# A delta rule kernel: the 4x4 diagonal blocks of a triangular inverse by shuffles and elementwise products in place of 32x32 matmuls

## The chip, the cores and the metric

One core of one Trainium2 chip runs the whole program. The metric is the time of one execution on the device in microseconds. The instructions of an engine run in the order in which they stand; the engines wait for each other by semaphores.

## The reference

The reference is one inference step of a trunk of two layers over 640 tokens (512 latent, 128 prompt). Each layer makes one projection whose columns feed three token mixers (a gated delta rule in both directions, an HGRN2 in both directions, windowed attention), merges the three, and ends in a gated MLP with a convolution. The change touches the delta rule, 4 heads of 128, by chunks of 64 tokens:

```python
decay = _masked_exp(incl, gc[..., :, None] - gc[..., None, :])
kb = k * beta[..., None]
m = jnp.where(strict, jnp.einsum('nbhid,nbhjd->nbhij', kb, k) * decay, 0.0)
t_inv = lax.linalg.triangular_solve(eye + m, jnp.broadcast_to(eye, m.shape),
                                    left_side=True, lower=True, unit_diagonal=True)
u = t_inv @ (v * beta[..., None])
w = t_inv @ (kb * jnp.exp(gc)[..., None])
...
v_new = u_n - jnp.einsum('bhck,bhkv->bhcv', w_n, s)
o = jnp.einsum('bhck,bhkv->bhcv', qg_n, s) + jnp.einsum('bhcs,bhsv->bhcv', qk_n, v_new)
s = s * jnp.exp(gl_n)[..., None, None] + jnp.einsum('bhck,bhcv->bhkv', kd_n, v_new)
```

## The kernel before

The main stream is the projection. It computes 128 columns for all 640 tokens at a time (a tile), from eight steps over the 1024 inputs (`k_steps`, L969; `mtile`, L976); each step is three pairs of fp32r matmuls of 256 and 384 columns, `mm<-hh,whi`, `mm<-hl,whi` and `mm<-hh,wlo`, since activations and weights are each split into a high and a low part. ScalarE (ACT) makes the high part of a weight tile, VectorE (DVE) the low part `wlo`, while the tile before is used. The side streams are generators that run beside it: two delta streams (`delta`, L1281; stream w = 0 takes batches 0, 2, 4, stream w = 1 batches 1 and 3; a batch below 4 is one head of the latent tokens, batch 4 all heads of the prompt), the HGRN streams, attention, and more. Their PSUM tiles are named `sd`, their SBUF slots `ex` and `sl`, their small tiles `sc_...`; `Cv`, `V`, `S` belong to the convolution that follows the projection of a delta head.

No scheduler of a compiler orders this. The planner (`drive`, L512; `step`, L500) keeps its own estimate of when each engine comes free (`_go`, L286, with a cost for each kind of instruction) and places a side stream's next piece, up to its `yield`, when its inputs are estimated to be there; else it places the next step of the main stream. Pieces of the convolutions wait in `aux` and are placed by `pump`. So the order in which every engine works is fixed when the program is built, and depends on the estimated costs. A stream can wait for an event or for free slots (`wait`, `room`); while the main stream waits, only side streams are placed. It waits at three kinds of places; the one after the last tiles of the mixer's projection is

```python
yield from c_tiles()
yield self.wait(("D", l, 0), ("D", l, 1))
```

(L2088 and L2089): both delta streams must have ended before it computes the gates.

In `delta` the inverse of each chunk's triangle, forward and backward at once, is built by doubling blocks, in 32x32 blocks that sit on the diagonal of 128 partitions (L1364 to L1399). `ath` holds the masked products of k with k and the decay, `XC` and `XTC` the inverse so far and its transpose. Blocks of two are made on DVE by a masked product with `bs` (beta of the token and its neighbour). Then four steps make blocks of 4, 8, 16 and 32; each is sixteen 32x32 matmuls, a masked product on DVE (L1388), sixteen more, a transpose and two subtractions on DVE:

```python
for i in range(1, 5):
    ...
    self.mul(phc..., pp..., bc(self.C(C_CP, 2)[:, 32 * i + 32:32 * i + 64], 1, 4))
    ...
    self.vtr(small, px)
    self.sub(yt, yt, blocks(px, m))
    self.sub(e, e, blocks(small, m))
```

Blocks of 64 follow with ACT copies between PE groups (L1401 to L1440). Then, in a batch below 4, a scan over four chunks goes from PE to DVE (`stt`, L371), to PE, to ACT, to PE, to DVE; batch 4 has no scan. `finish_tokens` (L1530) ends a batch: four squares on ACT, a reciprocal root of 4 elements a partition in eleven DVE instructions, a product over 512 columns, and four transposes on PE that need it.

Of the kernel before, what the change touches and what calls it, by code (L numbers as in the profile page):

```python
# [12 lines left out]
ALU = mybir.AluOpType  # L13
# [39 lines left out]
C_I, C_ONE, C_MISC, C_UI, C_LI, C_LS, C_US, C_CP, C_COS = 0, 1, 2, 3, 4, 5, 6, 7, 9  # L53
# [8 lines left out]
def shape_constants():  # L62
    c = np.zeros((128, N_CST), np.float32)
    p = np.arange(128)
    s, t = p[:, None], p[None, :]

    def put(i, a):
        c[:, i * 128:i * 128 + a.shape[1]] = a

    put(C_I, s == t)  # L70
    put(C_ONE, np.ones((128, 128)))
    put(C_UI, s <= t)
    put(C_LI, s >= t)
    put(C_US, s < t)
    put(C_LS, s > t)
    t32 = np.arange(32)[None, :]
    put(C_CP, np.concatenate([s % 32 == t32] + [(s % 32 // (2 << i) == t32 // (2 << i)) & (s % 32 >> i != t32 >> i)
                                                for i in range(5)], 1))
    misc = np.zeros((128, 128), np.float32)
    misc[:64, 2] = 1.0  # L80
    misc[64:, 3] = 1.0
    misc[:, 40] = p % 2 == 0
    misc[:, 41] = p % 2 == 1
    for g in range(4):
        for j in range(16):
            misc[32 * g + j, 8 + j] = 1.0
    for j in range(4):
        for e in range(2):
            misc[32 * j + e, 24 + 2 * j + e] = 1.0
    put(C_MISC, misc)  # L90
    nf = 16
    inv = (np.float32(10000.0) ** (-np.arange(nf, dtype=np.float32) / np.float32(nf))).astype(np.float32)
    pos = np.arange(TS)
    row, col = (pos // 64).astype(np.float32), (pos % 64).astype(np.float32)
    ang = np.where((p % 64 < 32)[:, None], row[None, :], col[None, :]).astype(np.float32) * inv[p % 16][:, None]
    put(C_COS, np.cos(ang.astype(np.float32)))
    put(C_SIN, np.sin(ang.astype(np.float32)) * np.where(p % 32 < 16, -1.0, 1.0).astype(np.float32)[:, None])
    return c
# [120 lines left out]
def bc(ap, axis, n):  # L219

    d = [list(x) for x in ap.ap]
    d.insert(axis, [0, n])
    return bass.AP(ap.tensor, ap.offset, d)
# [13 lines left out]
class Trunk:  # L237
# [325 lines left out]
    def setup(self):  # L563
# [13 lines left out]
        self.c_us, self.c_ls = C(C_US), C(C_LS)  # L577
        self.c_blk, self.c_pick = C(C_MISC)[:, 2:34], C(C_MISC)[:, 24:32]
        self.c_sum = C(C_MISC)[:, 8:24]
        self.c_par = C(C_MISC)[:, 40:42]  # L580
        self.hh = self.hp.tile([128, KD, T], F32R, name="hh")
        self.hl = self.hp.tile([128, KD, T], F32R, name="hl")
        self.S = [self.const.tile([128, 648], F32, name=f"S{j}") for j in range(2)]
# [696 lines left out]

    def delta(self, l, w, batches):  # L1281
        sc, nc = dict(self.sc), self.nc
        for name in ("ssk", "nk", "rk", "b0", "bs", "cq", "ss"):
            sc[name] = self.sc[name][:, w]
        sl = (self.extra, self.slots)
        P, X, XT, kd = (self.pair(*sl) for _ in range(4))
# [1 line left out]
        ath, ph = View(P, 0), View(P, 1)  # L1288
# [3 lines left out]
        for b in batches:  # L1292
# [27 lines left out]
            self.rsqrt(rk, ssk, nk)  # L1320
            self.mul(nk, ssk, rk)
            self.mul(ssk, rk, rk)
            b0 = sc["b0"]
            self.mul(b0, beta, bc(ssk, 1, 2))

            bs = sc["bs"]
# [41 lines left out]
            self.zero(x64)  # L1368
            XC, XTC = (xs.ap[:, o:o + 256].rearrange("p (d n) -> p d n", d=2) for o in (0, 256))
            c32, t32 = (a.rearrange("p d (c x) -> p d c x", c=4) for a in (XC, XTC))  # L1370
            self.mul(t32, bc(bc(self.C(C_CP)[:, 0:32], 1, 4), 1, 2), bc(b0, 3, 32))
            for g in range(4):
                r = slice(32 * g, 32 * g + 32)
                self.mul(phc[r].rearrange("p (c x) -> p c x", c=4), ath.c4[r, :, r], bc(self.C(C_CP)[r, 32:64], 1, 4))
            self.mul(c32, bc(phc.rearrange("p (c x) -> p c x", c=4), 1, 2), bc(bs, 3, 32))
            self.sub(XTC, XTC, XC)
            self.vtr(xs.ap[:, 0:256], xs.ap[:, 256:512])
            yield None
            for i in range(1, 5):
                m = 1 << i  # L1380
                pp = self.psd()[:, 0:128]
                e = mix(XC, m, 0)
                yt = mix(XTC, m, 1)
                for c in range(4):
                    for g in range(4):
                        r = slice(32 * g, 32 * g + 32)
                        self.mm(pp[r, c * 32:(c + 1) * 32], ath.c4[r, c, r], mix_chunk(e, c, m)[r])
                self.mul(phc.rearrange("p (c x) -> p c x", c=4), pp.rearrange("p (c x) -> p c x", c=4),  # L1388
                         bc(self.C(C_CP, 2)[:, 32 * i + 32:32 * i + 64], 1, 4))
                yield None  # L1390
                px = self.psd()[:, 0:128]
                for c in range(4):
                    for g in range(4):
                        r = slice(32 * g, 32 * g + 32)
                        self.mm(px[r, c * 32:(c + 1) * 32], phc[r, c * 32:(c + 1) * 32], mix_chunk(yt, c, m)[r])
# [3 lines that stand above are left out]
                yield None  # L1399
# [507 lines left out]
    def mixer(self, l, x):  # L1907
# [12 lines left out]
        sc = self.sc = {}  # L1920
        for name, shape in (("ab", [2, 2, 5, 4]), ("beta", [2, 5, 4]), ("g", [2, 5, 4]), ("gl", [2, 5, 4]), ("t0", [2, 5, 4]), ("t1", [2, 5, 4]),
                            ("t2", [2, 5, 4]), ("ex", [3, 2, 5, 4]), ("neg", [2, 5, 4]), ("ssk", [2, 4]), ("nk", [2, 4]), ("rk", [2, 4]),
                            ("b0", [2, 2, 4]), ("bs", [2, 2, 4]), ("cq", [2, 4]), ("ss", [2, 3, 4]), ("ssb", [3, 4]), ("ck", [3, 10]),
                            ("s8", [3, 5, 8]),
                            ("mx", [4]), ("ng", [4]), ("es", [4]), ("sm", [4])):
            sc[name] = mp.tile([128] + shape, F32, name="sc_" + name)
# [401 lines left out]
```

## Time and profile before

| what | us |
|---|---|
| median of three runs | 2674.06 |
| lowest and highest | 2673.45, 2674.49 |
| the profiled execution's own time | 2671.22 |
| its span, first to last instruction | 2669.4 |
| PE busy | 2634.9 |
| DVE busy | 1843.0 |
| ACT busy | 1130.8 |
| POOL busy | 114.4 |

The granted clock of TensorE was 1.000 over the whole span. The profile has a page with the busy time of each engine, the chain of work that ended last and the costliest groups; beside it, views of the trace answer for one stretch, one line or one group. In the rows, `x` gives how many records stand in one row; a 32x32 or 128x128 matmul of fp32 has two records, so a group of sixteen stands as x32. What stands in square brackets at a row's end is how long the engine was idle before it, and for whom it waited.

### The profile page before, as it was taken

What the parts mean: (1) busy time and instruction counts of PE and PEld (TensorE: products, weight loads), DVE (VectorE), ACT (ScalarE), POOL (GpSimd) and SP (SyncE); (2) the same over time, 40 slices, a digit from 0 to 9 for tenths busy, and PEclk for the clock granted to TensorE, in tenths of its full rate; (3) what the DMA queues carried; (4) which work ended last, traced back from release to release, by engine and by line L of the source; (5) the groups of instructions that cost most, each with busy time, mean ns of one, the idle gap of its engine ahead of it and who ended that gap; (6) DMA issues with size and microseconds to landing.
All of it is one profiled execution on the core that took longest, in us unless ns stands there. A gap on an engine that the chain in (4) does not pass through costs nothing.

```text
span 2669.4 us, 58665 instructions
## 1 busy us (share of the span) xinstructions
PE 2634.9 (99%) x23938; PEld 2534.1 (95%) x23938; DVE 1843.0 (69%) x4250; ACT 1130.8 (42%) x2577; POOL 114.4 (4%) x208
## 2 busy tenths in 40 slices
PE   8999999999999999999999999999999999999999
PEld 5999999999999999999999998999999999999999
DVE  6788865656765897988667888666564457546454
ACT  5555455544424432323345554645443334323232
POOL 1100110100000000000001001000000000000000
PEclk9999999999999999999999999999999999999999
DMA  8212222312444344444322112222222232222222
GB/s 270 73 40 58 65 75 80 112 53 60 134 132 131 100 141 154 151 149 148 108 77 75 44 49 63 65 71 66 56 64 68 76 115 68 77 74 69 83 74 81
DMA packets 365245, 243.49 MB, mean 91 GB/s; under 512 B 18069, under 2 KB 339137, under 8 KB 364848
## 3 DMA queue, kind: packets, MB, share of 16 engines
q1 hardware_dynamic: 355632, 213.70, 27.7%
q0 software_dynamic: 8912, 25.53, 2.9%
q8 instruction: 188, 3.08, 0.5%
q14 instruction: 81, 0.66, 0.1%
q10 hardware_dynamic: 432, 0.52, 0.1%
HBM read 225.79 MB, written 13.89 MB: 90 GB/s over the span
## 4 chain that ended last, share of the span: by engine, by line
PE 88%; DVE 7%; ACT 2%; issue 2%; DMA 1%; SPq 0%; ACTq 0%; DVEq 0%
PE mm L323 73%; PE sd L323 12%; PE sd L328 2%; DVE sl L358 1%; DVE ex L358 1%; DVE Cv L371 1%; ACT sl L348 1%; DMA ar<-in_ada_w_dram 1%; DVE acc L371 1%; DVE wlo L358 1%; DMA wraw<-in_w_up_dram 0%; DVE N L371 0%; SPq L433 0%; ACT ex L348 0%; DVE x L371 0%
## 5 line engine op out<-in xcount | busy, mean ns | idle before, releaser
L323 PE MATMUL mm<-hh,whi 128*128 128x256 f32 (+2 forms) x3696 | 868.7, 319 | 1.4 <-issue 0.7
L323 PE MATMUL mm<-hl,whi 128*128 128x256 f32 (+2 forms) x3696 | 840.4, 311 | 1.2 <-DVE hl L371 1.2
L323 PE MATMUL mm<-hh,wlo 128*128 128x256 f32 (+1 forms) x3632 | 834.8, 309 | 0.0
L323 PEld LDWEIGHTS mm<-hh,whi 128*128 128x128 f32 (+1 forms) x3696 | 646.1, 187 | 23.8 <-issue 15.4
L323 PEld LDWEIGHTS mm<-hl,whi 128*128 128x128 f32 (+1 forms) x3696 | 663.7, 187 | 4.0 <-DVE hl L371 1.8
L323 PEld LDWEIGHTS mm<-hh,wlo 128*128 128x128 f32 x3632 | 661.7, 188 | 0.0
L358 DVE TENSOR_TENSOR wlo<-wraw,whi 128x512 fp32r<-128x512 f32 x598 | 401.8, 681 | 302.6 <-ACT whi L348 301.8
L348 ACT ACTIVATE whi<-wraw 128x512 fp32r<-128x512 f32 x602 | 366.8, 618 | 306.7 <-PE mm L323 245.6
L371 DVE SCALAR_TENSOR_TENSOR Cv<-S,V,Cv 128x642 f32<-128x642 f32 x240 | 210.9, 886 | 2.3
L371 DVE SCALAR_TENSOR_TENSOR acc<-ar,cT,acc 128x512 f32<-128x512 f32 x252 | 176.8, 749 | 4.2 <-DMA ar<-in_ada_w_dram 4.0
L348 ACT ACTIVATE sl<-sl 128x512 f32<-128x512 f32 (+5 forms) x220 | 117.6, 545 | 143.5 <-DVE sl L358 103.3
L323 PE MATMUL mm<-fh,whi 128*128 128x256 f32 (+1 forms) x704 | 166.0, 311 | 1.8 <-DVE x L371 1.0
L323 PE MATMUL mm<-fl,whi 128*128 128x256 f32 (+1 forms) x704 | 165.0, 309 | 0.2
L323 PE MATMUL mm<-fh,wlo 128*128 128x256 f32 (+1 forms) x704 | 165.1, 309 | 0.0
L348 ACT ACTIVATE sl<-sd 128x512 f32<-128x512 f32 (+5 forms) x216 | 94.4, 451 | 161.7 <-PE sd L323 79.6
L323 PE MATMUL sd<-sl,sl 128*32 128x32 f32 (+4 forms) x3392 | 151.2, 228 | 6.3 <-DVE sl L358 5.1
L323 PEld LDWEIGHTS sd<-sl,sl 128*32 128x32 f32 (+3 forms) x3392 | 126.1, 129 | 26.8 <-issue 13.9
L358 DVE TENSOR_TENSOR sl<-sl,sl 128x512 f32<-128x512 f32 (+2 forms) x212 | 149.0, 741 | 3.3 <-ACT sl L348 2.0
L348 ACT ACTIVATE S<-mm 128x512 f32<-128x512 f32 x204 | 77.8, 434 | 155.0 <-PE mm L323 154.8
L371 DVE SCALAR_TENSOR_TENSOR x<-mm,mod,x 128x256 f32<-128x256 f32 (+1 forms) x192 | 74.6, 434 | 88.2 <-PE mm L323 83.8
L323 PEld LDWEIGHTS mm<-fh,whi 128*128 128x128 f32 x704 | 128.0, 189 | 4.2 <-issue 2.9
L323 PEld LDWEIGHTS mm<-fl,whi 128*128 128x128 f32 x704 | 128.1, 188 | 0.7 <-DVE fl L358 0.7
(280 smaller groups left out, 3121.6 us busy)
## 6 DMA issues: line engine op xcount, KB each, us to landing
wraw<-in_w_in_dram SPq DMA_DIRECT2D x264, 256.0 KB, 3.0
ar<-in_ada_w_dram SPq DMA_DIRECT2D x176, 256.0 KB, 3.5
wraw<-in_w_up_dram SPq DMA_DIRECT2D x176, 256.0 KB, 3.0
wraw<-in_w_down_dram SPq DMA_DIRECT2D x64, 256.0 KB, 3.0
wraw<-in_w_branch_dram SPq DMA_DIRECT2D x48, 256.0 KB, 3.0
wraw<-in_w_out_dram SPq DMA_DIRECT2D x32, 256.0 KB, 3.6
wraw<-in_w_down_dram SPq DMA_DIRECT2D x32, 192.0 KB, 2.6
x<-xspill POOLq DMA_DIRECT2D x16, 320.0 KB, 7.0
```

Source lines behind the costliest of these rows:

```text
L323: self.nc.tensor.matmul(out, lhsT, rhs, start=start, stop=stop)
L328: self.nc.tensor.transpose(out, in_, self.c_i[:k, :k])
L348: self.nc.scalar.activation(out=out, in_=in_, func=func, scale=scale, bias=bias, **kw)
L358: self.nc.vector.tensor_tensor(out, a, b, op=op)
L371: self.nc.vector.scalar_tensor_tensor(out=out, in0=a, scalar=s, in1=b, op0=op0, op1=op1)
```

## The change

The first of the four doubling steps, from blocks of two to blocks of four, is done on DVE without a matmul. The masks of the first two levels are applied in one product (`two`) to a copy of the diagonal blocks, one reduction sums it to 16 numbers a partition (`r4`), and shuffles between lanes, masks by a lane's parity in pairs (`c_pair`) and products of 4 or 8 elements (`q4`, `l4`, `z4`) make the block's four corner numbers (`zt`), which two products spread over 32 columns. The loop of matmuls begins with blocks of eight. Two masks and two constant columns are added, in tiles that the program loads already.

```diff
@@ shape_constants
-    put(C_CP, np.concatenate([s % 32 == t32] + [(s % 32 // (2 << i) == t32 // (2 << i)) & (s % 32 >> i != t32 >> i)
-                                                for i in range(5)], 1))
+    facing = [(s % 32 // (2 << i) == t32 // (2 << i)) & (s % 32 >> i != t32 >> i) for i in range(5)]
+    put(C_CP, np.concatenate([s % 32 == t32] + facing + [facing[1] & (s // 2 % 2 == d) for d in range(2)], 1))
...
+    misc[:, 42] = p // 2 % 2 == 0
+    misc[:, 43] = p // 2 % 2 == 1
@@ delta
-        for name in ("ssk", "nk", "rk", "b0", "bs", "cq", "ss"):
+        for name in ("ssk", "nk", "rk", "bo", "bs", "r4", "q4", "l4", "z4", "cq", "ss"):
             sc[name] = self.sc[name][:, w]
...
-            b0 = sc["b0"]
+            b0, off = sc["bo"][:, 0], sc["bo"][:, 1]
             self.mul(b0, beta, bc(ssk, 1, 2))
...
-            self.mul(t32, bc(bc(self.C(C_CP)[:, 0:32], 1, 4), 1, 2), bc(b0, 3, 32))
+
+            one = ph.ap[:, 256:384].rearrange("p (c x) -> p c x", c=4)
+            two = ph.ap[:, 0:256].rearrange("p (c i x) -> p c i x", c=4, i=2)
             for g in range(4):
                 r = slice(32 * g, 32 * g + 32)
-                self.mul(phc[r].rearrange("p (c x) -> p c x", c=4), ath.c4[r, :, r], bc(self.C(C_CP)[r, 32:64], 1, 4))
-            self.mul(c32, bc(phc.rearrange("p (c x) -> p c x", c=4), 1, 2), bc(bs, 3, 32))
+                self.vcopy(one[r], ath.c4[r, :, r])
+            self.mul(two, bc(one, 2, 2), bc(self.C(C_CP)[:, 32:96].rearrange("p (i x) -> p i x", i=2), 1, 4))
+            self.mul(t32, bc(bc(self.C(C_CP)[:, 0:32], 1, 4), 1, 2), bc(b0, 3, 32))
+            r4, (own, far), l4, z4 = sc["r4"], (sc["q4"][:, i] for i in range(2)), sc["l4"], sc["z4"]
+            self.rsum(r4.rearrange("p c i j -> p (c i) j"), ph.ap[:, 0:256].rearrange("p (a n j) -> p a j n", a=8, j=2))
+            self.mul(c32, bc(two[:, :, 0], 1, 2), bc(bs, 3, 32))
+            self.add(z4[:, 0, :, 0], r4[:, :, 0, 0], r4[:, :, 0, 1])
+            self.sub(XTC, XTC, XC)
+            self.stt(off, bc(z4[:, 0, :, 0], 1, 2), -1.0, bs, ALU.mult, ALU.mult)
+
+            a4, o4, u4 = r4[:, :, 1], z4[:, 1], z4[:, 2:4]
+            self.shuffle(o4, a4, [i ^ 1 for i in range(32)])
+            for t, m in ((far, 1), (own, 0)):
+                self.ts(t, sc["bo"][:, :, 0], self.c_pair[:, m:m + 1], ALU.mult)
+            for t, m in ((far, 0), (own, 1)):
+                self.stt(t, sc["bo"][:, :, 1], self.c_pair[:, m:m + 1], t, ALU.mult, ALU.add)
+            for j in range(2):
+                self.shuffle(l4[:, j], far, [i & 28 | (i & 2 ^ 2) + j for i in range(32)])
+            zz, zt = z4[:, 0], z4[:, 4]
+            self.mul(zz, a4, bc(own[:, 0], 2, 2))
+            self.mul(o4, o4, bc(own[:, 1], 2, 2))
+            self.add(zz, zz, o4)
+            for kind in range(2):
+                self.mul(u4[:, kind], zz, l4[:, :, kind].rearrange("p j c -> p c j"))
+            (ps_, pn_), (s1, _), (s2, _), (s0, _) = u4.ap
+            self.add(zt, u4[:, 0], bass.AP(u4.tensor, u4.offset + s1 + s0, [[ps_, pn_], [s2, 4], [-s0, 2]]))
+            for d in range(2):
+                self.mul(c32[:, d].rearrange("p c (n j) -> p c n j", j=2), bc(zt, 2, 16),
+                         bc(self.C(C_CP, 2)[:, 192 + 32 * d:224 + 32 * d].rearrange("p (n j) -> p n j", j=2), 1, 4))
             self.sub(XTC, XTC, XC)
             self.vtr(xs.ap[:, 0:256], xs.ap[:, 256:512])
             yield None
-            for i in range(1, 5):
+            for i in range(2, 5):
...
```

The planner counts the new instructions, so it sets another order in both layers, though none of its rules is edited. Three places follow, each as the order of the program lists it: line, operation, output and inputs, shape, and how many follow each other. First DVE, layer 0, first batch, the head of the inverse (`ex_684` before and `ex_688` after hold `XC` and `XTC`). Before:

```order
L358 TENSOR_TENSOR ex_684<-cst,sc_b_667 128x256
L358 TENSOR_TENSOR ex_692<-ex_692,cst 32x128 x4
L358 TENSOR_TENSOR ex_684<-ex_692,sc_bs 128x256
L358 TENSOR_TENSOR ex_684<-ex_684 128x256
L387 STREAM_TRANSPOSE ex_684<-ex_684 128x256
```

After, from the same place, the first twelve rows:

```order
L384 COPY ex_696<-ex_696 32x128 x4
L360 TENSOR_TENSOR ex_696<-ex_696,cst 128x256
L360 TENSOR_TENSOR ex_688<-cst,sc_bo 128x256
L410 TENSOR_REDUCE sc_r_668<-ex_696 128x16
L360 TENSOR_TENSOR ex_688<-ex_696,sc_bs 128x256
L360 TENSOR_TENSOR sc_z_671<-sc_r_668 128x4
L360 TENSOR_TENSOR ex_688<-ex_688 128x256
L373 SCALAR_TENSOR_TENSOR sc_bo<-sc_z_671,sc_bs 128x8
L394 STREAM_SHUFFLE sc_z_671<-sc_r_668 128x8
L378 TENSOR_SCALAR sc_q_669<-sc_bo,cst 128x8 x2
L373 SCALAR_TENSOR_TENSOR sc_q_669<-sc_bo,cst,sc_q_669 128x8 x2
L394 STREAM_SHUFFLE sc_l_670<-sc_q_669 128x8 x2
```

All of the new piece stands in one run on DVE, with no instruction of another stream in it.

Second PE, layer 1, the end of the delta streams (`sl_...` and `ex_...` are their slots, `cst` the unit matrix of a transpose). Before, the last row of a delta stream is a transpose of `finish_tokens` among main matmuls, 246 main matmuls ahead of the wait at L2089:

```order
L323 MATMUL mm<-hh,wlo 128x256
L323 MATMUL mm<-hh,wlo 128x384
L328 MATMUL sd_73<-cst,ex_15685 128x128 x4
L323 MATMUL mm<-hh,whi 128x256
L323 MATMUL mm<-hh,whi 128x384
```

After, the last twelve rows of a run of 44 rows (186 matmuls) that stands at that wait, and the main matmul behind it:

```order
L325 MATMUL sd_75<-sl_15559,ex_19517 128x128 x2
L325 MATMUL sd_72<-ex_19516,sl_15576 128x128 x2
L325 MATMUL sd_73<-ex_15617,sl_15568 128x128 x2
L325 MATMUL sd_74<-sl_15559,ex_19517 128x128 x2
L325 MATMUL sd_74<-st_15578,sl_15565 128x128
L325 MATMUL sd_74<-ex_15617,sl_15565 128x128 x3
L325 MATMUL sd_75<-ex_15617,sl_15565 128x128 x3
L325 MATMUL sd_75<-st_15578,sl_15565 128x128
L325 MATMUL sd_72<-ex_19516,sl_15576 128x128 x8
L330 MATMUL sd_73<-cst,sl_15569 128x128 x4
L330 MATMUL sd_74<-cst,sl_15559 128x128 x4
L325 MATMUL mm<-hh,whi 128x256
```

The end of batch 3's scan, its outputs and its transposes moved from among the main matmuls to behind the last of them.

Third PE, layer 0, where the main stream waits for slots. Before, the end of a run of 24 rows (66 matmuls) without a main matmul, and what follows:

```order
L323 MATMUL sd_75<-st_654,sl_648 128x128
L323 MATMUL sd_72<-ex_4080,ex_689 128x128 x4
L323 MATMUL sd_73<-ex_4080,ex_689 128x128 x4
L323 MATMUL sd_74<-sl_634,ex_3836 128x128 x2
L323 MATMUL mm<-hh,whi 128x256
```

After, the end of the like run, of 30 rows (94 matmuls):

```order
L325 MATMUL sd_75<-st_654,sl_648 128x128
L325 MATMUL sd_72<-ex_4102,ex_693 128x128 x8
L325 MATMUL sd_73<-sl_634,ex_3818 128x128 x2
L325 MATMUL sd_74<-ex_3817,sl_651 128x128 x2
L330 MATMUL sd_75<-cst,sl_635 128x128 x4
L330 MATMUL sd_72<-cst,sl_644 128x128 x4
L325 MATMUL mm<-hh,whi 128x256
```

The transposes of an HGRN batch's `finish_tokens` (`sl_635`), which stood after further main matmuls, now stand ahead of them, twelve 128x128 matmuls behind the batch's last product.

## Rows read from the trace of the kernel before

**Rows 1.** The page: busy time by engine, and the chain that ended last.
```profile
PE 2634.9 (99%) x23938; PEld 2534.1 (95%) x23938; DVE 1843.0 (69%) x4250; ACT 1130.8 (42%) x2577; POOL 114.4 (4%) x208
...
PE 88%; DVE 7%; ACT 2%; issue 2%; DMA 1%; SPq 0%; ACTq 0%; DVEq 0%
```

**Rows 2.** Stretches of layer 1's mixer: stretch, its length, busy us (instructions) by engine.
```profile
1540.00:1600.00 60.00, 58.18 (x954) 53.80 (x954) 54.86 (x146) 32.82 (x82) 4.43 (x7) 1.00 0.18 47
1600.00:1660.00 60.00, 57.19 (x748) 53.94 (x750) 51.08 (x144) 28.12 (x68) 9.31 (x17) 1.00 0.24 65
1720.00:1780.00 60.00, 60.00 (x685) 57.65 (x685) 38.58 (x101) 28.40 (x70) 5.31 (x10) 1.00 0.31 85
```

**Rows 3.** Waits of PE from 1480 to 1830 us: total us, times, longest.
```profile
PE sd L323 <- DVE sl L358: 5.0, 3, 1.8
```

**Rows 4.** Timeline: start us, length us, engine, line, operation, tiles, shape, count.
```profile
113.32 0.46 PE L323 MATMUL mm<-hh,wlo 128*128 128x256 f32 x2
...
113.71 0.45 PE L323 MATMUL sd<-ex,ex 32*32 32x32 f32 x32
...
114.09 0.56 PE L323 MATMUL mm<-hh,whi 128*128 128x256 f32 x2
114.24 0.29 DVE L358 TENSOR_TENSOR ex<-sd,cst 128x128 f32<-128x128 f32 x1
...
114.49 0.46 PE L323 MATMUL mm<-hl,whi 128*128 128x256 f32 x2
...
114.79 0.46 PE L323 MATMUL mm<-hh,wlo 128*128 128x256 f32 x2
...
115.70 0.32 DVE L387 STREAM_TRANSPOSE ex<-sd 128x128 f32<-128x128 f32 x1 [0.37 <-PE sd L323]
...
115.94 0.25 DVE L358 TENSOR_TENSOR ex<-ex,sd 128x128 f32<-128x128 f32 x1
...
116.12 0.28 DVE L358 TENSOR_TENSOR ex<-ex,ex 128x128 f32<-128x128 f32 x1
```

**Rows 5.** Groups of DVE by shape: count, busy us, mean ns, idle before.
```profile
L358 DVE TENSOR_TENSOR ex<-ex,cst 32x128 f32<-32x128 f32 x40 | 11.2, 281 | 0.4
...
L358 DVE TENSOR_TENSOR sl<-sl 128x256 f32<-128x256 f32 x14 | 5.9, 422 | 0.1
...
L382 DVE COPY ex<-ex 32x128 f32<-32x128 f32 x24 | 5.2, 218 | 0.3
...
L404 DVE TENSOR_REDUCE sc_mx<-sd 128x1 f32<-128x128 f32 x16 | 3.5, 283 | 0.6 <-PE sd L323 0.6
...
L392 DVE STREAM_SHUFFLE sc_bs<-sc_b 128x8 f32<-128x8 f32 x10 | 1.6, 160 | 0.0
```

**Rows 6.** Timeline of DVE, the reciprocal root of layer 0's first batch.
```profile
94.59 0.16 DVE L376 TENSOR_SCALAR sc_ssk<-sc_ssk 128x4 f32<-128x4 f32 x1
...
97.36 0.17 DVE L358 TENSOR_TENSOR sc_b<-sc_beta,sc_ssk 128x8 f32<-128x8 f32 x1
```

**Rows 7.** Timeline: a scan step and the end of a batch in layer 1.
```profile
1700.03 0.60 ACT L348 ACTIVATE ex<-sd 128x512 f32<-128x512 f32 x1 [2.06 <-PE sd L323]
...
1700.88 0.75 PE L323 MATMUL sd<-sl,ex 128*128 128x128 f32 x4 [0.45 <-DVE sl L371]
...
1701.16 0.32 ACT L348 ACTIVATE ex<-ex 128x128 f32<-128x128 f32 x1
...
1704.85 0.69 DVE L358 TENSOR_TENSOR ex<-ex,sc_ss 128x512 f32<-128x512 f32 x1
```

**Rows 8.** Timeline of PE in layer 0, the stretch without main matmuls.
```profile
353.16 1.04 PE L328 MATMUL sd<-cst,sl 128*128 128x128 f32 x8
...
360.60 2.17 PE L323 MATMUL sd<-sl,sl 128*128 128x128 f32 x18
362.61 0.39 PE L323 MATMUL sd<-st,sl 128*128 128x128 f32 x2
...
364.99 0.54 PE L323 MATMUL mm<-hh,whi 128*128 128x256 f32 x2
```

More of the change, by code (lines that the diff above doesn't have):

```diff
@@ L579, in setup @@
         self.c_sum = C(C_MISC)[:, 8:24]
-        self.c_par = C(C_MISC)[:, 40:42]
+        self.c_par, self.c_pair = C(C_MISC)[:, 40:42], C(C_MISC)[:, 42:44]
         self.hh = self.hp.tile([128, KD, T], F32R, name="hh")
@@ L1922, in mixer @@
                             ("t2", [2, 5, 4]), ("ex", [3, 2, 5, 4]), ("neg", [2, 5, 4]), ("ssk", [2, 4]), ("nk", [2, 4]), ("rk", [2, 4]),
-                            ("b0", [2, 2, 4]), ("bs", [2, 2, 4]), ("cq", [2, 4]), ("ss", [2, 3, 4]), ("ssb", [3, 4]), ("ck", [3, 10]),
+                            ("bo", [2, 2, 2, 4]), ("r4", [2, 4, 2, 2]), ("q4", [2, 2, 2, 4]), ("l4", [2, 2, 2, 4]), ("z4", [2, 5, 4, 2]), ("bs", [2, 2, 4]), ("cq", [2, 4]), ("ss", [2, 3, 4]), ("ssb", [3, 4]), ("ck", [3, 10]),
                             ("s8", [3, 5, 8]),
```

## The prediction

> **What bounds the kernel now.** I read the page's busy shares and its chain first [rows 1]. TensorE (PE) is busy 2634.9 of 2669.4 us, about 34 us are idle, and PE makes 88% of the chain that ended last, DVE 7%. So a PE instruction taken away counts at nearly its whole length, and DVE time counts only where it makes PE wait. Next I read the engines by stretch, in layer 1's mixer, where the delta streams, the HGRN streams and the conv taps all want DVE [rows 2]: PE is busy 58.18 and 57.19 of 60 us there, DVE 54.86 and 51.08 (91% and 85%); DVE is the second bound there, with only 5 to 9 us free in 60. By 1720 to 1780 us PE is full (60.00) and DVE down to 38.58: there the delta streams are done and the projection runs alone. In 1480 to 1830 us PE waits three times for one DVE line's products, 5.0 us in all, 1.8 the longest [rows 3]. That is the price of DVE being late today.
>
> **Removed from PE.** One step of the inverse has two groups of sixteen 32x32 matmuls, over 10 batches (two layers of five): 20 groups. A group that stands alone between main matmuls [rows 4]: the pair before it starts at 113.32, the group at 113.71, the next pair at 114.09 and the one after at 114.49, so 1.17 us for two pair distances, where an undisturbed pair follows the next at 0.30 (114.49 to 114.79). It costs 1.17 - 0.60 = 0.57 us. A group with another small group on both sides gives back only its own 0.38 from start to start (113.71 to 114.09). Twenty of them are 7.6 to 11.4 us; most stand alone among main matmuls, so I take **-10.5 us**.
>
> **Added to and removed from DVE.** Removed per batch: the masked product, the transpose and the two subtractions of that step, 0.29 + 0.32 + 0.25 + 0.28 = 1.13 us [rows 4], and four masked products of 32x128 that become four copies: 281 to 218 ns each, 0.25 us in all [rows 5]. Added: two more 128x256 element operations (the masked doubles, the second subtraction) at 0.42 each, two 128x128 ones at 0.28, the reduction, and fifteen operations on 4 or 8 elements a partition. The reduction of 256 elements has no row: one of 128 elements takes 283 ns [rows 5], twice that is 0.57, and I take 0.42, since a 128x256 operation of the other kind takes that. The fifteen have their neighbours in the reciprocal root of the same batch: 14 operations start between 94.59 and 97.36, 0.198 us each [rows 6], though each lasts only 0.16 to 0.17; the shuffle among them lasts 160 ns [rows 5]. So 0.84 + 0.56 + 0.42 + 15 x 0.2 = 4.8 us are added, 1.4 removed: **+3.4 us of DVE a batch, 34 us in all**, which is not time of the kernel as long as PE has other rows ahead.
>
> An operation on 8 elements a partition takes 160 ns and one on 256 takes 422 [rows 5]: 32 times the elements for 2.6 times the time, so nearly all of a small one is fixed cost. [...]
>
> **What moves.** The delta chain of one batch gets longer: the old step took 113.71 to 116.40, 2.7 us with its waits [rows 4], the new piece 4.8 - 0.25 = 4.6 us of DVE back to back, so at least 2 us a batch. The planner answers with another order, and the order is where the money is.
> Layer 1: before, the last PE row of a delta stream stands 246 main matmuls (some 37 us at 0.30 a pair) ahead of the point where the main stream waits for both delta streams (L2089). After, both streams' last batches (batch 4 in w = 0, batch 3 in w = 1) are still going there: 44 PE rows, 186 matmuls, stand with not one main matmul between them. PE works in order and the whole projection is queued behind these rows, so each dependence in this block is idle time. I walked it by rows. Its PE work is some 20 us (90 of the matmuls are 128x128; nine fp32 ones, two records each, take 2.01 us from 360.60 to 362.61 [rows 8], 0.22 apiece, and transposes less). The waits:
> (a) two transposes at the end of a batch wait for `finish_tokens`: the squares start on ACT at 1701.16, the normed product is done at 1704.85 + 0.69, so 4.4 us, and the copy or add before it is another 0.6 to 0.7, 5.05 us from the last product to the transpose [rows 7]. Batch 4's has 0.95 us of other PE rows in between, idle 4.0; batch 3's has 0.4 (the last rows before the projection goes on), idle 4.7.
> (b) batch 3's scan, three and a half steps of matmul, DVE or ACT, matmul: the trace shows 0.45 us of PE idle for one such wait, though other work stood between [rows 7]; eight of them are 3.6.
> (c) the tail of the inverse, ACT copies between 32x32 and 64x64 groups: 0.65 + 1.25 + 0.6, about 2.5.
> Together 14.8; with 12 if the streams overlap better than I walked them and 18 if DVE is also behind on arrival, **+15 us**.
> Layer 0: the main stream is blocked for slots near main matmul 1376 in a block of 94 matmuls; before, a like block of 66 ran from 353.16 to 364.99 with no idle in it [rows 8]. In the new block the HGRN transpose at its end has 2.8 us of PE work (twelve 128x128 matmuls) between it and the last product it depends on, and needs the same 5.05: **+2.3 us** (1 to 4).
> Elsewhere DVE is late a little more often, or, with the deltas moved, the three waits of layer 1 [rows 3] go: -3 to +6, I take 0.
> Everything after main matmul 9440 (attention, merge, FFN) has the same order; nothing there. The wider constant masks and the new small tiles add no instruction of weight: the constants come in the one load that is there.
>
> **The sum**: -10.5 + 15 + 2.3 = +6.8 us against the profiled run's own 2671.22 us. The profiled run lies 2.8 us under the median of the runs; so the sum added to the median gives **2680.9 us**.
>
> **Rivals.** *Same time*: the block's idle is only 10 to 11 and layer 0's one, since in the block both streams' rows alternate better than in my walk (ACT and DVE run ahead, main work no longer competes for them). Then -10.5 + 11 + 1 = +1.5, 2675.6. For it: during the block DVE has no weights to split, so its queue is short. Against: (a) alone is 8.7 and is a chain of 4 squares on ACT and 13 DVE instructions, which no free engine shortens.
> *Faster*, one mechanism: the three DVE waits in layer 1 [rows 3] go with the shifted streams and the block is covered. Its place is the wait at L2089: if the rows of batch 4 and 3 reach PE with their operands ready (the chains having run ahead on DVE and ACT while main matmuls still filled PE, so that only PE work is left), the block costs its PE work alone, which was to be done anyhow. Then -10.5 + 2 for what is left of the waits and -2 for layer 1's three, or 2663.6. The deciding point is whether batch 3's scan starts before the block; in the order its first scan row stands in the block, hence the low chance.
> *Clearly slower*: DVE saturates. In layer 1's mixer 5 delta batches bring 17 us of DVE to stretches that have 5 to 9 free in 60 [rows 2]; if the order leaves them in about 100 us, 3 to 6 us more of PE waits come, and the block starts with DVE behind, 18: -8 + 18 + 4 + 4 = +18, 2692. [...]
> *The change does not do what it says*: PE's count of 32x32 groups would stay; the order shows 20 groups fewer, so this is out.
>
> **How the numbers follow.** Forecast (2678 to 2686): 0.45. Same: 0.28. Clearly slower (2686 to 2694): 0.15. Faster: 0.12. The measurement tells about 0.2% (5.3 us) from no change, so under 2668.7 is faster and above 2679.4 slower. The forecast's lower edge falls under that line; with it slower is 0.58, same 0.30, faster 0.12. The range leaves out the faster rival and the far end of the slower one: 2668.5 to 2690.
>
> **What would show it.** In the profile after: 320 fewer 32x32 matmuls, which are 640 records, ten reductions of 128x256, some +34 us of DVE busy; a stretch of about 35 us late in layer 1's mixer with no `mm` record and PE busy about 20 of it, two idle pieces of 4 to 5 us in it ending on a transpose that waited for DVE; PE busy in total about 10 us less. Wrong would be: the stretch there with under 8 us idle (then the same or faster rival), or PE waits spread over the whole mixer (then DVE is the bound).

## The result, and the profile after

The changed kernel takes 2703.64 us (median; 2702.01 to 2706.21) where the kernel before takes 2674.27 in the same comparison: a ratio of 1.0113, interval 1.0099 to 1.0128, so about 30 us slower. Its profiled execution has a span of 2700.8 us, 31.4 more than before, at a mean granted clock of 0.994 (1.000 before).

The page of the changed kernel, its busy times by engine and the chain that ended last, answers [rows 1]:

```profile
PE 2640.6 (98%) x23298; PEld 2539.8 (94%) x23298; DVE 1867.5 (69%) x4440; ACT 1131.5 (42%) x2579; POOL 114.7 (4%) x208
...
PE 79%; DVE 10%; ACT 3%; issue 2%; DMA 0%; DVEq 0%; ACTq 0%; SPq 0%
```

PE's idle time, span less busy, went from 34.5 to 60.2 us: +25.7. And PE's busy time did not fall with the 640 records that went; it rose by 5.7. Both have to be explained. Windows of the changed kernel (stretch, its length, busy us and instructions by engine; the third number from the right is the granted clock) answer [rows 2]: the place in layer 0 where the main stream is blocked, the block at the end of layer 1's delta streams, and a part of it:

```profile
360.00:420.00 60.00, 55.06 (x614) 52.59 (x613) 36.96 (x105) 28.25 (x76) 7.63 (x12) 0.97 0.27 78
1742.00:1792.00 50.00, 35.33 (x373) 31.21 (x373) 24.39 (x95) 21.59 (x66) 5.29 (x9) 0.80 0.12 35
1765.00:1780.00 15.00, 10.94 (x39) 8.88 (x40) 5.45 (x15) 1.75 (x4) 0.54 (x1) 0.52 0.03 8
```

The last one: the granted clock is 0.52 over its 15 us. From 1765.64 to 1782.71 it is 0.50, below called the lower clock. In its profiled execution the kernel before shows 1.00 in every such stretch of the mixers. PE's waits in the whole execution of the changed kernel (total us, times, longest) answer [rows 3]:

```profile
PE sd L330 <- DVE sl L360: 8.8, 3, 4.8
PE sd L330 <- DVE ex L360: 5.9, 2, 3.5
PE sd L325 <- ACT ex L350: 5.5, 9, 1.2
...
PE mm L325 <- DVE wlo L360: 3.1, 2, 2.4
```

Line 330 is the transposes (L328 before). The rows of the block itself, start and length in us, show how it goes:

```profile
1761.52 0.71 PE L325 MATMUL sd<-ex,sl 128*128 128x128 f32 x4 [0.51 <-ACT ex L350]
...
1765.77 1.11 PE L330 MATMUL sd<-cst,ex 128*128 128x128 f32 x4 [3.54 <-DVE ex L360]
...
1768.19 1.22 PE L325 MATMUL sd<-sl,ex 128*128 128x128 f32 x4 [0.44 <-DVE sl L373]
...
1784.53 0.60 PE L330 MATMUL sd<-cst,sl 128*128 128x128 f32 x4
...
1785.46 0.31 ACT L350 ACTIVATE ex<-sl 128x128 f32<-128x128 f32 x1 [2.99 <-DVE sl L360]
...
1789.14 0.69 DVE L360 TENSOR_TENSOR sl<-sl,sc_ss 128x512 f32<-128x512 f32 x1
...
1789.98 1.09 PE L330 MATMUL sd<-cst,sl 128*128 128x128 f32 x4 [4.85 <-DVE sl L360]
...
1790.72 0.56 PE L325 MATMUL mm<-hh,whi 128*128 128x256 f32 x1
```

At 1765.77 the transposes of batch 4's `finish_tokens` have waited 3.54 us. From there on, matmul groups of the same shape take 1.22 us where that of 1761.52 took 0.71, and each waits again for the scan's step before. From 1784.53 on PE has nothing but the last transposes of batch 3: the chain from the first square on ACT to the end of the product on DVE is 1785.46 to 1789.83, 4.4 us, and PE waits 4.85 for it. The main matmuls begin again at 1790.72, 47 us after they stopped at 1743.4.

By the time at which the same main matmul starts, the changed kernel is 2 us late behind layer 0's mixer, 3 late where layer 1's mixer begins, 25 us ahead just before the block (the main matmuls are placed earlier there) and 31 late behind it.

### The profile page after: what moved, and what is told of

Same layout as the page of the kernel before. It is cut to its first block, busy times and chain, and to the rows that moved or that the text cites. A ratio compares the mean times of both kernels' runs of the same rounds, so it can differ in the third digit from the quotient of the medians.

```text
span 2700.8 us, 57598 instructions
## 1 busy us (share of the span) xinstructions
PE 2640.6 (98%) x23298; PEld 2539.8 (94%) x23298; DVE 1867.5 (69%) x4440; ACT 1131.5 (42%) x2579; POOL 114.7 (4%) x208
## 4 chain that ended last, share of the span: by engine, by line
PE 79%; DVE 10%; ACT 3%; issue 2%; DMA 0%; DVEq 0%; ACTq 0%; SPq 0%
PE mm L325 67%; PE sd L325 10%; PE sd L330 2%; DVE sl L360 2%; ACT sl L350 1%; DVE ex L360 1%; DVE Cv L373 1%; DVE wlo L360 1%; ACT ex L350 1%; DVE acc L373 1%; ACT whi L350 0%; DVE ex L384 0%; DVE sl L373 0%; DVE x L373 0%; ACT L350 0%
```

## The experiments

All comparisons below are with the kernel before on the same chip, which lay between 2674.4 and 2675.2 us. "Idle" is span less PE's busy time in the profiled execution.

| kernel | median us | PE busy | idle | DVE busy | clock |
|---|---|---|---|---|---|
| before | 2674.3 | 2634.9 | 34.5 | 1843.0 | 1.000 |
| changed | 2703.6 | 2640.6 | 60.2 | 1867.5 | 0.994 |
| e1, old order | 2697.5 | 2634.6 | 61.0 | 1865.0 | 0.997 |
| e2, new cost only | 2701.2 | 2647.8 | 53.0 | 1845.3 | 0.993 |
| e3, step left out | 2666.4 | 2627.6 | 36.4 | 1834.3 | 0.999 |
| e4, block filled | 2700.1 | 2647.7 | 50.0 | 1868.1 | 0.996 |
| e5, no small operations | 2678.1 | 2628.7 | 47.0 | 1848.6 | 0.999 |
| e6, spread | 2691.5 | 2638.4 | 52.1 | 1864.3 | 0.995 |
| e7, layer 1 in the old order | 2689.2 | 2633.8 | 53.8 | 1866.4 | 0.996 |
| e8, old order, fewer taps | 2694.7 | 2638.2 | 54.3 | 1847.4 | 0.994 |
| e9, before, fewer taps | 2674.3 | 2635.9 | 34.8 | 1825.5 | 0.999 |
| e10, POOL and spread | 2693.0 | 2637.0 | 54.0 | 1852.4 | 0.996 |
| e11, before, small operations | 2703.1 | 2645.4 | 53.4 | 1865.5 | 0.996 |
| e12, best of both | 2685.3 | 2633.7 | 49.3 | 1865.7 | 0.996 |

The theory at the start was that of the prediction, that the planner's new order exposes the end of the delta streams, with the fallen clock that the profile after shows on top. Its rival was that the new DVE operations cost the time in any order.

**The new work in the old order, and the old step left out.** Planning and issuing are taken apart: the planner reckons with the old step, whose instructions are not issued (`Null`), and the new piece is issued without being planned (`mute`). e3 has the ghost of the step alone, in the code of before.

```diff
+            self.nc = Null()
+            self.mul(t32, bc(bc(self.C(C_CP)[:, 0:32], 1, 4), 1, 2), bc(b0, 3, 32))
...
+            self.nc, self.mute = nc, True
             one = ph.ap[:, 256:384].rearrange("p (c x) -> p c x", c=4)
...
+            self.mute = False
             yield None
-            for i in range(2, 5):
+            for i in range(1, 5):
                 m = 1 << i
+                self.nc = Null() if i == 1 else nc
```

> The new DVE piece is computed as in the changed kernel, but the planner reckons with the old step, so every engine's other rows stand in the order of the kernel before; the 20 groups of 32x32 matmuls are gone. Theory (the loss is the new order: exposed chain at the wait for the delta streams, with a fallen clock behind it): the 44-row block is gone and the time is 2674 less 7 to 11 us of PE plus 0 to 6 us of waits for a busier DVE, 2663 to 2673 us. Rival (the new DVE operations themselves are too much for DVE, in whatever order): 2695 us or more. Rival (half and half): 2680 to 2690.

> The kernel before in its own order with the doubling step from blocks of two to four left out and nothing in its place (that part of the inverse is not computed). It measures what the 20 groups of 32x32 matmuls and their four DVE operations a batch are worth. By the prediction's term -10.5 us (7.6 to 11.4): 2663 to 2667. If PE groups of this size are mostly covered by waits that come anyway: 2670 or more.

Measured: e1 2697.5 us, ratio 1.0087 (1.0072 to 1.0102); e3 2666.4, ratio 0.9968 (0.9956 to 0.9979). The page of e3:

```profile
PE 2627.6 (99%) x23298; PEld 2529.0 (95%) x23298; DVE 1834.3 (69%) x4210; ACT 1130.3 (42%) x2577; POOL 114.7 (4%) x208
```

So the twenty groups and their DVE operations are worth 8.7 us of time, and 7.3 of PE's busy time, as the prediction's term says. And the theory on the order fell as the whole account, e1 being in its first rival's range: with the order of before, the block gone and the groups gone, the new piece costs 31 us more than leaving the step out. PE's waits in e1:

```profile
PE sd L336 <- DVE sl L371: 23.6, 12, 4.1
PE sd L336 <- DVE ex L371: 6.2, 6, 2.2
```

One of the twelve, in layer 0. First e1 (the piece begins at 140.76 and its last row is the transpose at 146.35):

```profile
140.76 0.92 DVE L395 COPY ex<-ex 32x128 f32<-32x128 f32 x4
...
145.17 0.17 DVE L371 TENSOR_TENSOR sc_z<-sc_z 128x8 f32<-128x8 f32 x1
...
146.35 0.45 DVE L400 STREAM_TRANSPOSE sl<-sl 128x256 f32<-128x256 f32 x1
...
146.90 1.20 DVE L371 TENSOR_TENSOR sl<-sl,sl 128x1024 f32<-128x1024 f32 x1
...
148.25 0.54 PE L336 MATMUL sd<-sl,sl 128*32 128x32 f32 x32 [2.53 <-DVE sl L371]
```

Then the same rows of the kernel before (the head begins at 136.99):

```profile
136.99 0.42 DVE L358 TENSOR_TENSOR sl<-cst,sc_b 128x256 f32<-128x256 f32 x1
...
139.44 0.45 DVE L387 STREAM_TRANSPOSE sl<-sl 128x256 f32<-128x256 f32 x1
...
139.99 1.20 DVE L358 TENSOR_TENSOR sl<-sl,sl 128x1024 f32<-128x1024 f32 x1
...
142.76 0.45 PE L323 MATMUL sd<-sl,sl 128*32 128x32 f32 x23
```

Right behind the transpose that ends the head, DVE has a product of an HGRN stream, which PE needs. Before, the head lasts to the product's start 3.0 us, the product is done at 141.19 and PE comes to its row at 142.76: 1.6 us to spare. In e1 the same stretch lasts 6.1 us (140.76 to 146.90), 3.1 longer; PE, without two groups of matmuls, comes 0.8 earlier against it; 1.6 to spare less 3.9 leaves it 2.3 us short, and the row shows a wait of 2.53. The product isn't part of the inverse. It stands behind it in DVE's one queue.

**The planner's order alone.** The kernel before, with the planner told of the new piece's DVE time and none of it issued.

```diff
+            self.nc, self.mute = Null(), False
+            one = ph.ap[:, 256:384].rearrange("p (c x) -> p c x", c=4)
...
+            self.vtr(xs.ap[:, 0:256], xs.ap[:, 256:512])
+            self.nc = nc
```

> The kernel before, all its instructions, none of the new ones; only the planner is told that the head of the inverse costs the new piece's DVE time as well, so that it sets an order like that of the changed kernel: at the wait for the delta streams a block of 57 rows without main matmuls, in layer 0 one of 48 rows. Theory (order): slower by 20 to 45 us, 2694 to 2720, with the granted clock under 1 in layer 1's block. Rival (the operations, not the order): 2674 to 2678.

Measured 2701.2 us, ratio 1.0098 (1.0083 to 1.0113). DVE is as busy as before (1845.3), and the time is 26 us longer, as the theory on the order said: 18.5 us more idle and 12.9 more busy. So an order like that of the changed kernel costs about as much as the piece does in the old one: the planner exchanged one loss for another. (The blocks without main matmuls are longer in e2, 57 and 48 rows, than in the changed kernel, 44 and 30; so 26 us is not the price of the changed kernel's own order.)

**What the clock takes.** Matmuls of no use fill PE's waits in the block of layer 1.

```diff
+    def fill(self, ps, n):
+        for _ in range(n):
+            self.nc.tensor.matmul(ps, self.hh[:, 0, 0:128], self.hh[:, 0, 0:512], start=True, stop=True)
...
         pt = self.psd()
+        self.fill(pt, n)
```

> The changed kernel with matmuls of no use put into the idle places of the block at the end of layer 1's delta streams: 16 and 22 of 512 columns ahead of the two transposes that end batches 4 and 3, two ahead of each scan step's matmuls of batch 3. They ask for nothing that is late. Theory (the clock falls because PE idles there, and the slow stretch behind it costs about 11 us): the granted clock stays at 1.00 through the block and the time falls to 2691 to 2696. Rival (the clock costs nothing, the chain on DVE and ACT is the whole time of the block): 2702 to 2706.

Measured 2700.1 us, ratio 1.0094 (1.0077 to 1.0111), 3.5 us under the changed kernel: neither theory's range. In the block itself the first theory's mechanism is there. Its window and some rows (those of `sd<-hh` are the filling):

```profile
1745.00:1787.00 42.00, 39.41 (x416) 32.61 (x415) 21.85 (x85) 21.09 (x66) 5.29 (x9) 1.00 0.16 43
```

```profile
1768.43 0.60 PE L325 MATMUL sd<-ex,sl 128*128 128x128 f32 x4
1768.80 0.71 PE L1569 MATMUL sd<-hh 128*128 128x512 f32 x2
1769.48 0.75 PE L325 MATMUL sd<-sl,ex 128*128 128x128 f32 x4
...
1786.29 0.60 PE L330 MATMUL sd<-cst,sl 128*128 128x128 f32 x4
1786.64 0.54 PE L325 MATMUL mm<-hh,whi 128*128 128x256 f32 x2
```

The clock is 1.00, the scan's groups take 0.60 to 0.75 us where they took 1.22, and the block lasts 41.5 us (1745.1 to 1786.64) where it lasted 47.3. So inside the block the clock costs 5.8 us and not 11. The rest is the chain on ACT and DVE: from the last row ahead of each pair of transposes to the transposes it is as long as in the changed kernel (5.39 and 5.46 us here, 5.38 and 5.45 there). Behind the block a wait of 1.95 us, which the changed kernel has with 0.59, takes part of it back; the mean granted clock of e4 is 0.996.

**How the loss goes with the length of the run, and whether spreading it helps.** e5 leaves the fifteen small operations out of e1; e6 issues the same operations as e1 at the three places where the old step had its DVE work.

```diff
 e5
-            self.stt(off, bc(z4[:, 0, :, 0], 1, 2), -1.0, bs, ALU.mult, ALU.mult)
...
+            zt = bc(self.C(C_MISC)[:, 44:46], 1, 4)
 e6
                 self.nc = nc
+                if i == 1:
+                    self.mute = True
+                    self.stt(off, bc(z4[:, 0, :, 0], 1, 2), -1.0, bs, ALU.mult, ALU.mult)
...
+                    self.mute, m = False, 1 << i
                 yield None
...
+                if i == 1:
+                    self.mute = True
+                    for d in range(2):
...
+                    self.sub(XTC, XTC, XC)
+                    self.vtr(xs.ap[:, 0:256], xs.ap[:, 256:512])
+                    self.mute = False
```

> As the run in the old order (2697.5), but without the fifteen operations on 4 or 8 elements (the corner numbers are put as zero, so that part of the inverse is not computed): the copies, the doubled mask product, the reduction, the two spreading products and the second subtraction stay. A head of the inverse then takes about 3.7 us of DVE in one run where it was 2.8 before and 6.0 in the run in the old order. Theory A (each us that DVE is longer there costs PE about one): the loss against the left-out step falls with the length, 10 x 1 us or so, 2675 to 2682. Theory B (the number of small operations does not matter, having the piece there does): 2690 or more. Theory C (a threshold: PE is hit only when the run outlasts the slack of the order): 2666 to 2671.

> The same operations as in the run in the old order, none left out, PE in the same order, but the new piece is not one run of 6 us on DVE: it stands in three parts (about 2.9, 2.2 and 1.3 us) at the places where the old step had its head, its masked product and its transpose, with other streams' DVE rows between. Theory A (PE loses by rows of other streams that queue behind one long run of DVE): most of the 31 us go, 2668 to 2680. Theory B (DVE has no time left in the mixers, so its sum counts and not its pieces): 2692 to 2700, as in one run.

e5: 2678.1 us, ratio 1.0016 (1.0006 to 1.0025). e6: 2691.5, ratio 1.0060 (1.0045 to 1.0075). Over the left-out step (2666.4), 14.3 us more DVE busy cost 11.7 us, and 30.7 more cost 31.1: near one for one, with no sign of a threshold. Of these, 10.6 and 24.6 us are PE's idle time; the other 1.1 and 7.0 are more busy time of the same matmuls. e5 is where theory A put it. In three parts (e6) the same work still costs 25.1, between the two ranges. Its waits:

```profile
PE sd L336 <- DVE sl L371: 8.2, 8, 2.0
...
PE sd L336 <- DVE ex L371: 4.6, 5, 1.9
PE sd L336 <- DVE ex L400: 3.9, 4, 2.6
...
PE sd L336 <- DVE sl L400: 2.7, 3, 1.5
```

The waits for the products (L371) are down to 8.2 and 4.6 us, but waits for the delta stream's own transposes (L400) come, 6.6 us in seven. Part of what is taken off the rows that queue behind comes back in the chain of the inverse, since that is done no earlier. At this point I read e5 and e6 as "DVE's sum counts".

**Whether it is DVE's sum.** One tap of each of the 24 delta convolutions is planned and not issued, in e1 (e8) and in the kernel before (e9); in e10, the spread run, eight small and spreading products and sums and one product of 128x256 stand on POOL.

```diff
 e8, e9
+                self.nc = Null() if width == 5 and j == 4 else nc
 e10
-            self.mul(t32, bc(bc(self.C(C_CP)[:, 0:32], 1, 4), 1, 2), bc(b0, 3, 32))
+            self.pmul(t32, bc(bc(self.C(C_CP)[:, 0:32], 1, 4), 1, 2), bc(b0, 3, 32))
...
+    def pmul(self, out, a, b):
+        self.nc.gpsimd.tensor_tensor(out, a, b, op=ALU.mult)
```

> The run in the old order (2697.5; new piece in one run on DVE, PE in the order of before), with one of the five taps of each of the 24 delta convolutions planned but not issued (their last tap is left out of the result): 24 DVE instructions of about 0.89 us less, 21 us of DVE in the same stretches, none of it in the delta chain's inverse. Theory A (the sum of DVE work in the mixers is what PE waits for): 0.8 to 1.0 us of time for each us, 2676 to 2682. Theory B (the inverse's own chain became too long for the order, whatever else DVE does): 2692 or more.

> The kernel before with the same 24 taps left out and nothing else changed: its DVE is 21 us shorter, PE as it was. If PE waits for DVE in the mixers of the kernel before as well at the full rate: 2655 to 2660. If that order has slack, so that only its few waits for DVE (about 8 us in all the mixers) can go: 2668 to 2674.

> The piece in three parts as in the spread run (2691.5), but six of the small products and sums, the two spreading products and one 128x256 product stand on POOL: DVE is some 18 us shorter in all, the chain of the inverse is longer by hops between engines. Theory A (sum of DVE): 2674 to 2680. Theory B (chain): 2692 to 2720.

e8: 2694.7 us (ratio 1.0076, 1.0059 to 1.0092). e9: 2674.3 (0.9999, 0.9990 to 1.0009). e10: 2693.0 (1.0066, 1.0051 to 1.0081). None is in the range that goes with DVE's sum. The same waits in e8:

```profile
PE sd L336 <- DVE sl L371: 21.6, 11, 4.1
...
PE sd L336 <- DVE ex L371: 2.8, 4, 1.8
```

In e8 DVE lost 17.6 us of busy time, and PE's waits for those products 2.0 and 3.4. PE's idle time fell by 6.7 us in all, but its busy time rose by 3.6 (the mean granted clock is 0.994 and not 0.997), and the time fell by 2.8. So taking DVE work away elsewhere does give something where PE waits for DVE, but well under half of it even as idle time. In e9 DVE lost 17.5 and the time nothing. In e10 DVE has 12 us less than in e6 and the time is no shorter; the small operations are slow on POOL, as its group shows (count, busy us, mean ns; the same product takes 164 ns on DVE in the changed kernel):

```profile
L374 POOL TENSOR_TENSOR sc_z<-sc_z,sc_l 128x8 f32<-128x8 f32 x20 | 10.7, 556 | 0.8
```

**Lateness at one place.** What is left is mainly where the time is put, and less how much DVE has to do. The last test adds it to the kernel before and takes nothing away.

```diff
+            self.mute = True
+            self.mul(sc["dm"][:, 0], b0, bs)
+            for n in range(14):
+                self.mul(sc["dm"][:, 1 - n % 2], sc["dm"][:, n % 2], bs)
+            self.mute = False
             self.sub(XTC, XTC, XC)
             self.vtr(xs.ap[:, 0:256], xs.ap[:, 256:512])
```

> The kernel before with all its matmuls and its order, and in each batch fifteen operations of 8 elements a partition on a scratch tile, each on the result of the last, unplanned, ahead of the transpose that ends the inverse's head: some 2.2 to 3 us more of DVE in one run, ten times, and no matmul taken away. The tap run showed that DVE's sum is not what PE waits for. Theory B' (every us that DVE is late at this place reaches PE, since the planned order has next to no slack behind it, once in a batch): 20 to 30 us slower, 2694 to 2704. Theory C (PE waits only because the two groups of matmuls are gone and it arrives earlier): 2674 to 2684.

Measured 2703.1 us, ratio 1.0109 (1.0092 to 1.0126): +28.7. DVE in the first batch, and PE's waits:

```profile
112.04 0.16 DVE L369 TENSOR_TENSOR sc_dm<-sc_b,sc_bs 128x8 f32<-128x8 f32 x1
112.24 2.78 DVE L369 TENSOR_TENSOR sc_dm<-sc_dm,sc_bs 128x8 f32<-128x8 f32 x14
...
115.39 0.45 DVE L398 STREAM_TRANSPOSE ex<-ex 128x256 f32<-128x256 f32 x1
...
115.89 0.45 PE L334 MATMUL sd<-ex,ex 32*32 32x32 f32 x32 [1.96 <-DVE ex L398]
```

```profile
PE sd L334 <- DVE ex L398: 11.5, 6, 3.0
...
PE sd L334 <- DVE sl L398: 5.0, 3, 2.1
```

The run of fifteen lasts 3.0 us, ten times: 30 us put in, 28.7 us out, with every matmul of the old step in its place. So PE need not come earlier for it to wait. That the two numbers are so near is in part chance: PE's idle time rose by 18.9 us, under two thirds of what was put in, and its busy time by 10.5, though it has the same matmuls; 20.4 us of that busy time lie in six stretches at the lower clock (pairs 0.53 us apart, as at 1577.71 and 1668.88), where the profile of before has none in the mixers. The largest waits are for the transpose of the inverse (L398) here, as they are for the HGRN products in e1.

**The best of both orders.**

> The new operations in both layers, the changed kernel's order in layer 0 and the old order in layer 1. By the times at which the same main matmul starts, layer 0 loses 3 us in the changed kernel's order and 16 in the old one, layer 1 loses 29 in the changed kernel's and 11 in the old. If the layers add up: 2674 + 3 + 11 = 2688, 2684 to 2692. If the old order's loss in layer 1 depends on what layer 0 hands on: 2697 or more.

> The new operations in both layers: layer 0 in the changed kernel's order (+3 us there), layer 1 in the old order with the piece in three parts (+8.5 us there in the spread run, by the time of the same main matmul). If the layers add up: 2686, 2683 to 2689, the least of the kernels with the new piece and still over the kernel before. If an order can hide the piece: 2674 or less.

```diff
+            ghost = l == 1
+            if ghost:
+                self.nc = Null()
...
-            for i in range(2, 5):
+            for i in range(1 if ghost else 2, 5):
```

Both plan the old step in layer 1 alone; e12 also issues the piece there in the three parts of e6. e7: 2689.2 us, ratio 1.0053 (1.0037 to 1.0070). e12: 2685.3, ratio 1.0038 (1.0025 to 1.0051). Both are in the ranges: the layers add up as reckoned, and the least loss found with the new piece is 10.8 us. No version that beats the kernel before was found.

## Why the prediction was wrong

The direction was right, and the block in layer 1 came as forecast; the size and the range (2668.5 to 2690) were wrong, because the clock had no term and the waits outside the two blocks were put at nothing. The difference of the two spans, 31.4 us, against the terms of the sum:

- **Removed from PE, -10.5** (7.6 to 11.4). Measured -7.3 in PE's busy time and -8.7 in time (e3). Inside its bounds by time, at the low end: "most stand alone among main matmuls" was wrong. Between the main matmuls of the kernel before, twelve of the twenty groups that e3 lacks stand with other small groups and eight alone; at the prediction's own prices that is 9.1.
- **The block in layer 1, +15** (12 to 18). PE's idle time in it is 14.5 us: the two ends of a batch 3.54 and 4.85 (forecast 4.0 and 4.7), the scan's eight waits 0.44 to 0.51 each, and three ahead of them 0.92, 0.57 and 0.86 (2.35 together, where the inverse's tail was forecast at 2.5). This term holds. Its PE work was taken as 20 us and is 32.7; halving what runs at the lower clock leaves some 25.
- **Layer 0's block, +2.3** (1 to 4). The transposes wait 3.55, and two waits for ACT ahead of them are 0.65 and 0.51: 4.7, over the end. The chain from the last product to the transposes took 7.0 us (366.36 to 373.37) and not 5.05: in ACT's queue two copies for another chain, which waited for PE until 368.18, stood ahead of the squares, so these began at 368.94 though their operand was there at 366.99.
- **Elsewhere, 0** (-3 to +6). Idle time rose by 25.7 - 14.5 - 4.7 = 6.5 us, with single waits up to 2.4 for transposes and for `wlo`.
- **The clock, no term at all.** This is the step that failed most. PE's busy time should have fallen by 7.3 and rose by 5.7: 13.0 us are matmuls at the lower clock. The profile of the changed kernel says the same directly. The granted clock is 0.50 in five stretches, and PE is busy in 26.5 us of them (the second, the fourth and the sum):

```profile
1670.07:1673.48 3.41, 3.41 (x16) 3.41 (x15) 1.00 (x2) 3.29 (x4) 0.00 (x0) 0.50 0.43 113
...
1765.64:1782.71 17.07, 13.65 (x52) 11.59 (x53) 4.84 (x15) 2.89 (x8) 0.54 (x1) 0.50 0.05 15
...
sum 30.71, PE 26.47 PEld 24.12 DVE 14.45 ACT 12.75 POOL 0.54; mean PE 5.29 PEld 4.82 DVE 2.89 ACT 2.55 POOL 0.11
```

  If the same work took half of that at the full clock, as the 0.50 suggests, it would be 13.2 us less. By this estimate some 7 us belong to the block in layer 1 (e4 measured 5.8), about 1 to the main matmuls behind it, and 1.5 to 1.7 each to the waits of 3.55 (layer 0's block), 2.40 and 2.38 us. With the two of the block these are all the waits of over 2 us behind the kernel's start, and behind each the granted clock was 0.50: for 3.0 to 3.4 us behind four of them, for 16.9 behind that of 3.54.

  In the profile of the kernel before, a wait of 1.60 us leaves the next pairs at 0.30 us distance:

```profile
1643.13 0.46 PE L323 MATMUL sd<-sl,sl 128*32 128x32 f32 x32 [1.60 <-DVE sl L358]
...
1643.92 0.46 PE L323 MATMUL mm<-hl,whi 128*128 128x256 f32 x2
1644.22 0.46 PE L323 MATMUL mm<-hh,wlo 128*128 128x256 f32 x2
```

  In e1, after a wait of 1.91 us, pairs follow at 0.54:

```profile
126.25 0.45 PE L336 MATMUL sd<-ex,ex 32*32 32x32 f32 x32 [1.91 <-DVE ex L371]
...
128.00 0.73 PE L336 MATMUL mm<-hh,whi 128*128 128x256 f32 x2
128.54 0.73 PE L336 MATMUL mm<-hl,whi 128*128 128x256 f32 x2
```

  But it is not the length of the wait alone. In e3 the same row as in the kernel before, after the same 1.60 us, is followed by pairs at 0.53 for 3.4 us:

```profile
1636.65 0.46 PE L334 MATMUL sd<-sl,sl 128*32 128x32 f32 x32 [1.60 <-DVE sl L369]
...
1638.10 0.73 PE L334 MATMUL mm<-hh,whi 128*128 128x256 f32 x2
1638.63 0.73 PE L334 MATMUL mm<-hl,whi 128*128 128x256 f32 x2
```

  So every wait in the mixers of the kernel before that I priced by, 1.8 us at most, was one behind which the granted clock stayed at 1.00 in that one execution, and the two of 4 to 5 us that I forecast were longer than all of them. The waits of before said nothing of what comes behind longer ones, so the forecast block should have carried a price for its own matmuls as well: in the trace after, groups of the same shape take 1.22 us for 0.71 there, and e4 puts it at 5.8 us in the block.

With 14.5 + 4.7 + 6.5 + 13.0 - 7.3 the sum is 31.4. The forecast was 6.8: of the missing 24.6 us the clock is 13.0, the waits elsewhere 6.5, the groups 3.2 and layer 0's block 2.4, with 0.5 too much in layer 1's block. With the clock priced right and the rest as forecast the sum would have been 2693.9, still 10 short.

Two sentences on the way were wrong as well. "The order is where the money is" took the planner's new order for the whole cause: e1 shows that the piece in the order of before loses 23 us against before, and e12 that a mixture still loses 11. And "+34 us of DVE, which is not time of the kernel as long as PE has other rows ahead" (the busy time rose by 24.5; the new 128x8 operations that do not need the one just before them start 0.07 to 0.15 us apart and not 0.2) looked at whether PE has rows ahead, when the question was how soon PE comes to a row that needs something behind the piece. In the example that is 1.6 us. How much it is at each of the other places was not measured; that 18.9 of the 30 us in e11 reach PE as idle time suggests that it is little at most of them.

My rival of a saturated DVE gave 2692 and came nearer to the measured time, by luck: e9 shows no gain from a smaller sum on DVE and e8 a small one, so that the sum is not what binds. The rivals of the same time and of a faster kernel needed the chains to run ahead of PE; in the block they did not (waits of 3.54 and 4.85 us).

What stays open: what decides whether the clock falls behind a wait of 1.6 to 2.5 us, and whether a planner with wider margins could hide a piece of this length; neither was tried.

## What to carry to other kernels

Where an order is laid out so that each row meets its operand just in time, time put on another engine was not hidden by that engine's idle share (DVE is busy 69% of the span before): ask, for each run of added instructions, which row stands next in that queue, who waits for it and with how much to spare. Here twenty groups of matmuls were worth 8.7 us, and 3 us of delay in each of ten places cost 28.7, about two thirds of it as waits and one third as matmuls at the lower clock. A forecast wait on PE that is longer than those of the kernel before needs this second price, and as a range: behind waits of 1.6 to 2.5 us here came at one place nothing (pairs 0.30 us apart) and at another 3.4 us at the lower clock (pairs 0.53 to 0.54 apart).

## What the runs showed of the hardware that I had not expected

The length of a wait of PE did not decide by itself whether the granted clock fell behind it. It fell for 3.4 us behind one of 1.60 us in e3 (1637.92 to 1641.33), and not behind the same wait in the kernel before; behind one of 1.91 us in e1 (127.14 to 130.55), and not behind those of 2.22 and 2.43 us in e1 (pairs 0.30 apart behind 1503.33 and 1476.99) or of 1.96 and 2.05 us in e11 (pairs 0.30 apart behind 115.89 and 1655.36). Other executions of the kernel before show a mean granted clock of 0.998 to 1.000. What else differs between these places no run here took apart. Fifteen dependent operations of 8 elements on DVE take 0.2 us each (2.98 us from 112.04 to the end of the row at 112.24), while independent ones of the same size in the new piece start down to 0.07 us apart (144.42 to 144.49 in e1), though each is recorded with 0.16 us. A 128x8 product on POOL took 556 ns where DVE takes 164.
